# Two RWKV edits in a hybrid diffusion layer: 32x32 products that alternate between row halves, and zero-padded low parts of the small ranks

## The chip, the cores and the metric

The kernel runs on one core of a Trainium2 chip. The metric is the device time of one execution in microseconds (us). Below, PE is the matrix engine, PEld its weight loads, DVE the vector engine, ACT the scalar engine, POOL the GpSimd engine, SP the engine whose queue issues the DMAs.

## The reference

Two layers over 256 context and 512 latent tokens of width 1024. The even layer runs latent attention beside eight RWKV-7 heads of width 64, in both directions. What the change touches is the RWKV part:

```
w_log = -softplus(-(w0[d] + tanh(xw) @ w2[d])) - 0.5      # small rank 64 -> 512
a     = sigmoid(a0[d] + xa @ a2[d])                       # small rank 64 -> 512
def step(s, inp):                                         # per token, per head, per direction d
    r_t, w_t, k_t, v_t, kk_t, a_t = inp
    sa = einsum('bhij,bhj->bhi', s, -kk_t)
    s = s*w_t[:,:,None,:] + sa[...,None]*(kk_t*a_t)[:,:,None,:] + v_t[...,None]*k_t[:,:,None,:]
    return s, einsum('bhij,bhj->bhi', s, r_t)
```

Everything is float32 in and out.

## The kernel before

The token scan is done in 12 chunks of 64 tokens. In a chunk the recurrence is a unit triangular 64x64 system, and its inverse is formed ahead of the chain that walks through the chunks. The heads go in four pairs, p = 0 to 3, and two pairs share one chain, q = 0 (p 0 and 1) and q = 1 (p 2 and 3).

For each pair, `features(p)` projects r, k and v from the 1024-wide input (matmuls `acc<-h,whi` and `acc<-h,wlo`: every weight is split into a rounded high part and a low part, each in the one-pass format fp32r), then forms decay and learning rate from the small ranks. Their input `xla[n]` holds 64 rows of the high part and, in the other half, 64 rows of the low part of tanh(xw) (n = 0) or xa (n = 1). Two products make one result: `lhi` (128 rows, L626) and the weights' low part `llo` (64 rows, the half `H[n]`, L627). For 2 ranks, 2 directions and 4 pairs these are 16 accumulators, each with four matmuls: 256 and 512 columns by `lhi`, 256 and 512 by `llo`.

`rwkv_prep` multiplies the chunk matrices (`gk<-ar,bkt`) and copies what the inverse needs into `LS` and `PB`. `rwkv_inverse(p-1)` runs after it: DVE transposes `LS` into `I` (L738), POOL inverts the 32x32 diagonal blocks in 30 steps (L744, L746), DVE transposes the result into `PN` and `TT` (L751 to L754), and PE joins the two halves of each 64x64 inverse by two 32x32 products per chunk, row half and direction: `iv<-PN,PB` into bank `b`, copied by ACT to `w1` (L763), then `iv<-TT,w` into `b2`, copied to `TT` (L768), which a DMA writes to the record `sp_rec` (L770). The row halves are `Q`: rows 0 to 31 with 32 to 63, and rows 64 to 95 with 96 to 127. Before, all 12 chunks of one half stand ahead of the 12 of the other, and the copy of `b2` stands between the halves.

`rwkv_chain` then takes 12 steps for q = 0 and q = 1, each starting with loads of the record and of v (L800, L802). It overlaps with the attention's projections and heads; the rest (output projection, feed-forward, the whole odd layer) is dense matrix work from about 720 us on.

No order is written out by hand: the tile framework takes the program as written, places each instruction on its engine's in-order queue when its inputs are ready by its own cost estimate, and guards tiles by semaphores. A changed dependence in one place can therefore move instructions in others. A tile name without a number of buffers has one buffer, and a new writer waits for the last reader of the old contents.

Of the kernel before, what the change touches and what calls it, by code (L numbers as in the profile page):

```python
# [10 lines left out]
F32 = mybir.dt.float32  # L11
F32R = mybir.dt.float32r
AF = mybir.ActivationFunctionType
ALU = mybir.AluOpType
# [3 lines left out]
P = 128  # L18
# [10 lines left out]
NCH = 12  # L29
# [181 lines left out]
def hybrid_kernel(ctx: ExitStack, tc: tile.TileContext, a, out):  # L211
    nc = tc.nc
# [11 lines left out]
    def T(pool, shape, tag, bufs=1, dt=F32):  # L224
        uid[0] += 1
        return PL[pool].tile(shape, dt, tag=tag, bufs=bufs, name=f"{tag}_{uid[0]}")
# [26 lines left out]
    tt = nc.vector.tensor_tensor  # L253
# [247 lines left out]
    xla = [T("pa", [P, NTOK], f"xla{n}", 1, F32R) for n in range(2)]  # L501
# [28 lines left out]
    H = (slice(0, 64), slice(64, P))  # L530
    ALL = slice(0, P)
    SC = 96 ** -0.5
    ps = acc()
# [23 lines left out]
    ps = acc()  # L557
# [4 lines left out]
    ps = acc()  # L562
# [23 lines left out]
    for q in range(2):  # L586
        EC.append(T("misc", [P, 2, 2, NCH], f"EC{q}"))
        REC.append(tc.dram_tile([P, NCH, 2, 2, RECW], F32, name=f"sp_rec{q}"))
        VD.append([tc.dram_tile([64, NCH, 2, 2, CH], F32, name=f"sp_v{q}{m}") for m in range(2)])

    def features(p):
        r, k, v = [project(3 * p + b) for b in range(3)]
        vt = PJ()
# [16 lines left out]
                dma(dst[:, 2 + hh::-2, 1], src[:, 0:2])  # L610
                dma(dst[:, 10 + hh:3:-2, 1], src[:, 2:6])
        whi = [T("pa", [P, 2, P], f"lhi{n}", 1, F32R) for n in range(2)]
        wlo = T("pa", [P, 2, P], "llo", 1, F32R)
        for n in range(2):
            raw = T("pa", [P, 2, P], "lraw", 2)
            for m in range(2):
                dma(raw[H[m]], a["lora"][H[n], :, p * P:(p + 1) * P])
            nc.scalar.copy(whi[n], raw)
            tt(out=wlo[H[n]], in0=raw[H[n]], in1=whi[n][H[n]].bitcast(F32), op=ALU.subtract)
        sig, av = [], []  # L620
        for d in range(2):
            for n, (base, lst) in enumerate((("w0_", sig), ("a0_", av))):
                t = PJ()
                ps = acc()
                for (po, t0, nn, _) in SEG2:
                    mm(ps[:, po:po + nn], lhsT=whi[n][:, d], rhs=xla[n][:, t0:t0 + nn], start=True, stop=False)  # L626
                    mm(ps[:, po:po + nn], lhsT=wlo[H[n], d], rhs=xla[n][H[n], t0:t0 + nn], start=False, stop=True)  # L627
                act(t if d == 0 else t[:, ::-1], ps[:, PO:], AF.Sigmoid, bias=col(f"{base}{d}", p))
                lst.append(t)
        sq = PJ()  # L630
        act(sq, k, AF.Square, scale=col("k_k", p))
        ps = acc()
# [8 lines left out]
        ps = acc()  # L641
# [51 lines left out]
    Q = [(slice(64 * q, 64 * q + 32), slice(64 * q + 32, 64 * q + 64)) for q in range(2)]  # L693
# [40 lines left out]
    def rwkv_inverse(p, LS, PB):  # L734

        I = T("pp", [P, 32, 32], "I", 2)
        TT = T("pp", [P, 32, 64], "TT", 1)
        nc.vector.transpose(I.rearrange("p t s -> p (t s)"), LS.rearrange("p t s -> p (t s)"))  # L738
        Jf = T("pp", [P, 384], "w1", 2)
        eng = nc.gpsimd if INV_POOL[p] else nc.vector  # L740
        for m in range(1, 31):
            n = 31 - m
            tmp = Jf[:, :n * m].rearrange("p (t s) -> p t s", s=m)
            eng.tensor_tensor(out=tmp, in0=I[:, m + 1:, m:m + 1].to_broadcast([P, n, m]),  # L744
                              in1=I[:, m:m + 1, :m].to_broadcast([P, n, m]), op=ALU.mult)
            eng.tensor_tensor(out=I[:, m + 1:, :m], in0=I[:, m + 1:, :m], in1=tmp, op=ALU.add)  # L746
        nc.gpsimd.affine_select(out=I, in_=I, pattern=[[1, 32], [-1, 32]], compare_op=ALU.is_gt, fill=0.0,
                                base=0, channel_multiplier=0)
        nc.gpsimd.memset(I.rearrange("p t s -> p (t s)")[:, 0:1024:33], 1.0)
        PN = T("pp", [P, 32, 32], "PN", 1)  # L750
        nc.vector.transpose(PN, I.rearrange("p t s -> p s t"))  # L751
        for r0, r1 in Q:
            nc.vector.transpose(TT[r0, :, :32].rearrange("p i t -> p t i"), I[r0])
            nc.vector.transpose(TT[r1, :, 32:].rearrange("p i t -> p t i"), I[r1])  # L754
            nc.gpsimd.memset(TT[r1, :, :32], 0.0)
        for d in range(2):
            b = T("iv", [P, 512], "iv", 1)[:, :384].rearrange("p (c x) -> p c x", x=32)
            w1 = T("pp", [P, 384], "w1", 2).rearrange("p (c x) -> p c x", x=32)
            for r0, r1 in Q:
                for c in range(NCH):  # L760
                    mm(b[r1, c], lhsT=PB[r0, d * NCH + c], rhs=PN[r0, :, d * NCH + c], start=True, stop=True)
            for r0, r1 in Q:
                nc.scalar.copy(w1[r1], b[r1])  # L763
            b2 = T("iv", [P, 512], "iv", 1)[:, :384].rearrange("p (c x) -> p c x", x=32)
            for r0, r1 in Q:
                for c in range(NCH):
                    mm(b2[r0, c], lhsT=w1[r1, c], rhs=TT[r1, d * NCH + c, 32:], start=True, stop=True)
                nc.scalar.copy(TT[r0, d * NCH:d * NCH + NCH, 32:], b2[r0])  # L768
            for cs_, st_ in CMAP[d]:
                dma(REC[p // 2][:, st_, d, p % 2, 448:512], TT[:, d * NCH + cs_.start:d * NCH + cs_.stop])  # L770
# [179 lines left out]
    for tb in range(6):  # L950
        b = bank()
        n = 0
# [442 lines left out]
    ps = acc()  # L1395
# [230 lines left out]
```

## Time and profile before

| | us |
|---|---|
| median of 3 runs (2283.03 to 2285.35) | 2283.06 |
| the profiled execution | 2277.27 |
| its span, first to last instruction | 2275.6 |
| PE busy | 2103.0 (92%) |
| DVE busy | 1348.8 (59%) |
| ACT busy | 927.6 (41%) |
| POOL busy | 497.1 (22%) |

All that the change names lies between 30 and 505 us. A timeline row merges neighbours of one kind: start, time from the first start to the last end, engine, line, operation, output<-inputs, shape, count, and in brackets the idle time ahead of it with what ended it. A full float32 matmul shows as two records, an fp32r matmul as one. A matmul's recorded time includes its way through the array, so consecutive ones overlap in the record, and what one costs in a row of many is the distance of starts.

### The profile page before, as it was taken

The page shows a single profiled execution, that of the slowest core. Times are in us where ns is not written, and L with a number is a line of the kernel's source. Part 1 is how long each engine was busy: PE and PEld are TensorE (multiplying, and loading weights), DVE is VectorE, ACT ScalarE, POOL GpSimd, SP SyncE. Part 2 cuts the span into 40 slices and gives each one's busy share as a digit, 9 for nine tenths or more (in the row PEclk, how much of TensorE's full clock was granted, in tenths as well). Part 3 has the DMA queues.
Part 4 walks back from the last instruction along what each step waited for, and adds up shares of the span by engine and source line. Part 5 has one row for each costly group of instructions (what it writes and reads, how often), then busy time and mean ns, then how long its engine had stood idle before and what let it go on. Part 6 is the DMA issues. An engine that isn't in the chain of part 4 may idle for free.

```text
span 2275.6 us, 33862 instructions
## 1 busy us (share of the span) xinstructions
PE 2103.0 (92%) x13558; PEld 1654.7 (73%) x13558; DVE 1348.8 (59%) x2081; ACT 927.6 (41%) x1434; POOL 497.1 (22%) x484
## 2 busy tenths in 40 slices
PE   5988899798899999999999998898888999999997
PEld 3666668686555778888888886786565667888886
DVE  5466865666677556445354454678975556554555
ACT  4345663532245244223132335544344345332434
POOL 0027586621133010000000004342641230000000
PEclk9899899699999999999999999999888999999999
DMA  8477677659861432221211223313426032223231
GB/s 307 110 196 200 176 207 200 208 161 313 256 225 42 148 133 71 61 66 56 74 53 59 75 60 112 97 48 116 132 66 170 31 105 84 93 94 101 84 116 61
DMA packets 181069, 282.58 MB, mean 124 GB/s; under 512 B 63328, under 2 KB 118656, under 8 KB 177840
## 3 DMA queue, kind: packets, MB, share of 16 engines
q1 hardware_dynamic: 180912, 280.42, 40.7%
q8 instruction: 107, 1.75, 0.3%
q14 instruction: 50, 0.41, 0.1%
HBM read 225.43 MB, written 47.33 MB: 120 GB/s over the span
## 4 chain that ended last, share of the span: by engine, by line
PE 64%; DVE 6%; DMA 4%; ACT 4%; issue 2%; SPq 0%; DVEq 0%; POOL 0%; ACTq 0%; POOLq 0%
PE acc L267 49%; PE sd L267 3%; PE wo L267 2%; PE b L267 2%; PE ab L267 2%; PE o L267 2%; DVE E L1354 1%; DMA u<-sp_v 1%; DMA E<-sp_ac 1%; PE ax L267 1%; ACT L416 0%; DMA f<-sp_q 0%; DMA wraw<-w_out 0%; PE mb L267 0%; PE ad L267 0%
## 5 line engine op out<-in xcount | busy, mean ns | idle before, releaser
L267 PE MATMUL acc<-s,whi 128*128 128x512 f32 (+1 forms) x3104 | 762.3, 356 | 2.4 <-ACT s L463 2.4
L267 PEld LDWEIGHTS acc<-s,whi 128*128 128x128 f32 x3104 | 545.1, 188 | 94.3 <-ACT s L463 6.1
L267 PE MATMUL acc<-s,wlo 128*128 128x512 f32 (+1 forms) x1552 | 460.6, 357 | 0.0
L267 PE MATMUL acc<-h,whi 128*128 128x256 f32 (+2 forms) x1248 | 321.6, 371 | 15.4 <-ACT p L635 4.9
L325 ACT CAST whi<-wraw 128x1024 fp32r<-128x1024 f32 (+5 forms) x228 | 210.2, 923 | 284.3 <-PE acc L267 203.9
L267 PEld LDWEIGHTS acc<-s,wlo 128*128 128x128 f32 x1552 | 290.5, 188 | 46.7 <-DVE wlo L326 0.7
L267 PEld LDWEIGHTS acc<-h,whi 128*128 128x128 f32 (+1 forms) x1248 | 223.0, 196 | 67.9 <-issue 15.6
L326 DVE TENSOR_TENSOR wlo<-wraw,whi 128x1024 fp32r<-128x1024 f32 (+5 forms) x205 | 219.2, 1072 | 40.0 <-ACT whi L325 39.4
L381 DVE SCALAR_TENSOR_TENSOR s<-acc,pv,s 128x511 f32<-128x511 f32 (+1 forms) x132 | 87.0, 659 | 245.3 <-ACT s L380 244.4
L380 ACT ACTIVATE s<-acc,pv 128x512 f32<-128x512 f32 (+1 forms) x132 | 93.5, 708 | 231.8 <-PE acc L267 220.5
L484 DVE SCALAR_TENSOR_TENSOR x<-acc,mods,x 128x512 f32<-128x512 f32 (+1 forms) x136 | 79.4, 621 | 176.5 <-PE acc L267 176.4
L267 PE MATMUL acc<-h,wlo 128*128 128x256 f32 (+2 forms) x624 | 179.8, 362 | 0.0
L434 POOL TENSOR_TENSOR f<-f,f 128x768 f32<-128x768 f32 (+1 forms) x24 | 31.3, 1305 | 629.9 <-ACT f L429 622.4
L267 PEld LDWEIGHTS acc<-h,wlo 128*128 128x128 f32 (+1 forms) x624 | 120.3, 196 | 21.7 <-issue 5.2
L383 DVE SCALAR_TENSOR_TENSOR s<-acc,pv,s 128x511 f32<-128x511 f32 (+1 forms) x132 | 87.2, 660 | 4.3
L1173 POOL TENSOR_TENSOR s<-w,s 128x256 f32<-128x256 f32 x6 | 5.0, 857 | 382.4 <-ACT s L416 382.4
L387 ACT CAST s<-s 128x768 fp32r<-128x768 f32 (+1 forms) x44 | 32.0, 727 | 109.4 <-DVE s L1146 109.4
L744 POOL TENSOR_TENSOR w<-I 128x30 f32<-128x30 f32 (+14 forms) x120 | 69.8, 582 | 30.7 <-PE iv L267 12.9
L326 POOL TENSOR_TENSOR wlo<-wraw,whi 128x1024 fp32r<-128x1024 f32 x23 | 62.8, 2734 | 58.5 <-ACT whi L325 55.0
L746 POOL TENSOR_TENSOR I<-I,w 128x30 f32<-128x30 f32 (+14 forms) x120 | 71.9, 599 | 9.1
L1354 DVE TENSOR_SCALAR E<-E,acm 128x128 f32<-128x128 f32 x128 | 61.1, 546 | 16.9 <-ACT G L1351 16.9
L719 DVE TENSOR_TENSOR W<-gk,con 64x512 f32<-64x512 f32 x48 | 32.8, 683 | 55.9 <-ACT PB L718 55.5
(389 smaller groups left out, 3375.0 us busy)
## 6 DMA issues: line engine op xcount, KB each, us to landing
aw<-ada SPq DMA_DIRECT2D x96, 512.0 KB, 6.1
wraw<-up SPq DMA_DIRECT2D x88, 512.0 KB, 3.5
rec<-sp_rec SPq DMA_DIRECT2D x24, 1024.0 KB, 11.4
wraw<-w_in SPq DMA_DIRECT2D x47, 512.0 KB, 3.8
wraw<-down SPq DMA_DIRECT2D x40, 384.0 KB, 3.1
sp_rec<-tg SPq DMA_DIRECT2D x24, 384.0 KB, 3.4
E<-sp_ac SPq DMA_DIRECT2D x16, 512.0 KB, 6.6
x<-xT SPq DMA_DIRECT2D x16, 384.0 KB, 6.0
```

Of the source, the lines that this page charges most:

```text
L267: ins = nc.tensor.matmul(o, lhsT=lhsT, rhs=rhs, start=start, stop=stop, skip_group_check=shared)
L325: nc.scalar.copy(hi[:, :kt], raw[:, :kt])
L326: (eng or tt)(out=lo[:, :kt], in0=raw[:, :kt], in1=hi[:, :kt].bitcast(F32), op=ALU.subtract)
L380: act(o[rows, t0:t0 + n], ps[rows, po:po + n], AF.Identity, scale=w1, bias=b)
L381: stt(out=o[rows, t0 + 1:t0 + n], in0=ps[rows, po:po + n - 1], scalar=w0, in1=o[rows, t0 + 1:t0 + n], op0=ALU.mult, op1=ALU.add)
L383: stt(out=o[rows, t0:t0 + n - 1], in0=ps[rows, po + 1:po + n], scalar=w2, in1=o[rows, t0:t0 + n - 1], op0=ALU.mult, op1=ALU.add)
L387: nc.scalar.copy(hi, src)
L484: stt(out=x[:, t0:t0 + n], in0=ps[:, po:po + n], scalar=mods[:, c6 * 8 + m, c:c + 1], in1=x[:, t0:t0 + n], op0=ALU.mult, op1=ALU.add)
L719: tt(out=w[hk], in0=b[hk].rearrange("p c (a t) -> p c a t", a=2), in1=mk[hk].rearrange("p (a t) -> p a t", a=2).unsqueeze(1).to_broadcast( ...
L744: eng.tensor_tensor(out=tmp, in0=I[:, m + 1:, m:m + 1].to_broadcast([P, n, m]), in1=I[:, m:m + 1, :m].to_broadcast([P, n, m]), op=ALU.mult)
L746: eng.tensor_tensor(out=I[:, m + 1:, :m], in0=I[:, m + 1:, :m], in1=tmp, op=ALU.add)
L1354: ts(out=e[:, h], in0=e[:, h], scalar1=acm[:, c, h0 + h:h0 + h + 1], scalar2=0.0, op0=ALU.subtract, op1=ALU.min)
```

## The change

Three edits. The 32x32 products of both kinds loop over chunks outside and over row halves inside, so that neighbours belong to different halves; both copies of `b2` now stand behind all 24 products. The low parts of the small ranks get two tiles `llo0` and `llo1` of 128 rows, whose unused half POOL sets to zero once at the start; the product then takes all 128 rows (the zero rows add nothing). The staging tile `lraw` goes from two buffers to one.

```
+    llo = [T("pa", [P, 2, P], f"llo{n}", 1, F32R) for n in range(2)]
+    for n in range(2):
+        nc.gpsimd.memset(llo[n][H[1 - n]].bitcast(F32), 0.0)
...
-        wlo = T("pa", [P, 2, P], "llo", 1, F32R)
         for n in range(2):
-            raw = T("pa", [P, 2, P], "lraw", 2)
+            raw = T("pa", [P, 2, P], "lraw", 1)
             for m in range(2):
                 dma(raw[H[m]], a["lora"][H[n], :, p * P:(p + 1) * P])
             nc.scalar.copy(whi[n], raw)
-            tt(out=wlo[H[n]], in0=raw[H[n]], in1=whi[n][H[n]].bitcast(F32), op=ALU.subtract)
+            tt(out=llo[n][H[n]], in0=raw[H[n]], in1=whi[n][H[n]].bitcast(F32), op=ALU.subtract)
...
-                    mm(ps[:, po:po + nn], lhsT=wlo[H[n], d], rhs=xla[n][H[n], t0:t0 + nn], start=False, stop=True)
+                    mm(ps[:, po:po + nn], lhsT=llo[n][:, d], rhs=xla[n][:, t0:t0 + nn], start=False, stop=True)
...
-            for r0, r1 in Q:
-                for c in range(NCH):
+            for c in range(NCH):
+                for r0, r1 in Q:
                     mm(b[r1, c], lhsT=PB[r0, d * NCH + c], rhs=PN[r0, :, d * NCH + c], start=True, stop=True)
             for r0, r1 in Q:
                 nc.scalar.copy(w1[r1], b[r1])
             b2 = T("iv", [P, 512], "iv", 1)[:, :384].rearrange("p (c x) -> p c x", x=32)
+            for c in range(NCH):
+                for r0, r1 in Q:
+                    mm(b2[r0, c], lhsT=w1[r1, c], rhs=TT[r1, d * NCH + c, 32:], start=True, stop=True)
             for r0, r1 in Q:
-                for c in range(NCH):
-                    mm(b2[r0, c], lhsT=w1[r1, c], rhs=TT[r1, d * NCH + c, 32:], start=True, stop=True)
                 nc.scalar.copy(TT[r0, d * NCH:d * NCH + NCH, 32:], b2[r0])
```

The order of instructions changes on every engine from the first `lraw` on. Three places matter below. The first is DVE's queue at the features of p = 0; the `llo` rows are the low parts of p = 1, `p_852` or `p_855` is the running sum of the decay that everything after it needs. Before:

```order
L619 TENSOR_TENSOR llo_1358<-lraw_1359,lhi_203_1356 64x256
L640 SCALAR_TENSOR_TENSOR p_841<-f_631,pv_71,f_693 128x768
L661 SCALAR_TENSOR_TENSOR p_852<-scanm_116,p_805 128x768
L661 SCALAR_TENSOR_TENSOR p_874<-scanm_116,p_819 128x768
L619 TENSOR_TENSOR llo_1358<-lraw_1364,lhi_204_1357 64x256
L644 TENSOR_TENSOR f_755<-acc_843,f_755 128x768
L638 SCALAR_TENSOR_TENSOR p_833<-f_693,nkc_348,p_833 128x768
```

and now:

```order
L623 TENSOR_TENSOR llo_96_573<-lraw_1361,lhi_204_1359 64x256
L644 SCALAR_TENSOR_TENSOR p_844<-f_635,pv_71,f_697 128x768
L665 SCALAR_TENSOR_TENSOR p_855<-scanm_116,p_808 128x768
L665 SCALAR_TENSOR_TENSOR p_877<-scanm_116,p_822 128x768
L648 TENSOR_TENSOR f_759<-acc_846,f_759 128x768
L642 SCALAR_TENSOR_TENSOR p_836<-f_697,nkc_348,p_836 128x768
L682 SCALAR_TENSOR_TENSOR p_808<-p_815,p_836 128x768
L682 SCALAR_TENSOR_TENSOR p_822<-p_829,p_836 128x768
L623 TENSOR_TENSOR llo_97_574<-lraw_1366,lhi_205_1360 64x256
L683 TENSOR_TENSOR p_808<-p_808,p_855 128x768
```

The first subtraction stays ahead of the sums, but its tile is now read by rank n = 0 alone; the second one moved four places back. The second place is PE's queue at the join of p = 2 and the first chain step of q = 0 (`b_3934`, `b_3955`); `acc_5414` is the sum of squares of the attention's kv rank. Before:

```order
L267 MATMUL iv_3226<-PN_3218,PB_2214 32x32 x24
L267 MATMUL iv_3254<-TT_3153,w_455_3227 32x32 x12
L728 MATMUL gk_3145<-con_70,bkt_2939 128x128 x4
L267 MATMUL iv_3254<-TT_3153,w_455_3227 32x32 x12
L267 MATMUL acc_5414<-f_5417,ones_72 128x256
L267 MATMUL acc_5414<-f_5417,ones_72 128x512
L267 MATMUL iv_3282<-PN_3218,PB_2214 32x32 x24
L267 MATMUL b_3934<-u_3911,rec_3910 64x64 x8
L267 MATMUL iv_3310<-TT_3153,w_458_3283 32x32 x12
L267 MATMUL b_3934<-rs_3943,rec_3910 64x64 x8
L267 MATMUL iv_3310<-TT_3153,w_458_3283 32x32 x12
```

and now:

```order
L732 MATMUL gk_3145<-con_70,bkt_2939 128x128 x4
L267 MATMUL iv_3226<-PN_3218,PB_2215 32x32 x24
L267 MATMUL b_3934<-u_3911,rec_3910 64x64 x8
L267 MATMUL iv_3254<-TT_3153,w_453_3227 32x32
L267 MATMUL b_3934<-rs_3943,rec_3910 64x64 x8
L267 MATMUL iv_3254<-TT_3153,w_453_3227 32x32 x23
L267 MATMUL acc_5414<-f_5417,ones_72 128x256
L267 MATMUL acc_5414<-f_5417,ones_72 128x512
L267 MATMUL b_3955<-u_3911,rec_3910 64x64 x8
L267 MATMUL iv_3282<-PN_3218,PB_2215 32x32 x24
```

The chain's first step stands between the two kinds of joins, the second kind runs as one piece but for its first product, and the kv sum stands behind it. The third place is DVE's queue at the same time: `I_3393<-LS` is the start of the inverse of p = 3, `PN_3218` and `TT_3153` the transposes of p = 2. Before:

```order
L751 STREAM_TRANSPOSE PN_3218<-I_3152 128x1024
L753 STREAM_TRANSPOSE TT_3153<-I_3152 32x32x32
L754 STREAM_TRANSPOSE TT_3153<-I_3152 32x32x32
L753 STREAM_TRANSPOSE TT_3153<-I_3152 32x32x32
L754 STREAM_TRANSPOSE TT_3153<-I_3152 32x32x32
L719 TENSOR_TENSOR W_3122<-gk_3123,con_70 64x512
L722 TENSOR_TENSOR tg_3121<-gk_3123,con_70 64x4x64
L434 TENSOR_TENSOR f_5417<-f_5415,f_5417 128x768
L738 STREAM_TRANSPOSE I_3393<-LS_2963 128x1024
```

and now:

```order
L723 TENSOR_TENSOR W_3122<-gk_3123,con_70 64x512
L726 TENSOR_TENSOR tg_3121<-gk_3123,con_70 64x4x64
L742 STREAM_TRANSPOSE I_3393<-LS_2963 128x1024
L723 TENSOR_TENSOR W_3122<-gk_3134,con_70 64x512
L726 TENSOR_TENSOR tg_3121<-gk_3134,con_70 64x4x64
L755 STREAM_TRANSPOSE PN_3218<-I_3152 128x1024
L757 STREAM_TRANSPOSE TT_3153<-I_3152 32x32x32
L758 STREAM_TRANSPOSE TT_3153<-I_3152 32x32x32
L757 STREAM_TRANSPOSE TT_3153<-I_3152 32x32x32
L758 STREAM_TRANSPOSE TT_3153<-I_3152 32x32x32
```

The transposition that starts p = 3 moved ahead of the five of p = 2.

## Rows read from the trace of the kernel before

**Rows 1.** The page: span, and busy time, share and instructions of PE.

```profile
span 2275.6 us, 33862 instructions
PE 2103.0 (92%) x13558; PEld 1654.7 (73%) x13558; DVE 1348.8 (59%) x2081; ACT 927.6 (41%) x1434; POOL 497.1 (22%) x484
```

**Rows 2.** Stretches: length; busy PE, PEld, DVE, ACT, POOL; granted clock; DMA share; GB/s.

```profile
90.00:250.00 160.00, 137.54 (x778) 96.56 (x777) 96.28 (x121) 83.75 (x153) 70.89 (x83) 0.89 0.68 181
250.00:404.00 154.00, 145.62 (x1158) 114.08 (x1157) 100.37 (x114) 77.45 (x146) 106.18 (x149) 0.95 0.72 187
404.00:448.00 44.00, 32.44 (x365) 25.92 (x366) 26.87 (x33) 23.70 (x43) 23.02 (x40) 0.59 0.79 238
448.00:500.00 52.00, 51.53 (x483) 43.37 (x481) 36.33 (x44) 21.46 (x43) 19.68 (x31) 0.88 0.46 141
```

**Rows 3.** Groups by form on PE, 0 to 700 us: records, busy, mean ns.

```profile
L267 PE MATMUL iv<-PN,PB 32*32 32x32 f32 x384 | 21.5, 228 | 0.3 <-DVE PN L751 0.3
L267 PE MATMUL iv<-TT,w 32*32 32x32 f32 x384 | 18.5, 210 | 5.1 <-ACT TT L768 3.6 <-ACT w L763 1.5
L267 PE MATMUL acc<-xla,llo 64*128 64x512 f32 x16 | 8.8, 551 | 0.0
```

**Rows 4.** PE's timeline: one accumulator of the small ranks, and what follows.

```profile
312.79 0.38 PE L267 MATMUL acc<-xla,lhi 128*128 128x256 f32 x1
313.10 0.38 PE L267 MATMUL acc<-xla,llo 64*128 64x256 f32 x1
...
314.27 0.55 PE L597 MATMUL bkp<-con,f 128*128 128x128 f32 x3
```

**Rows 5.** PE's timeline: 128-row projections, then a run of 64-row products.

```profile
395.94 0.85 PE L267 MATMUL acc<-h,whi 128*128 128x256 f32 x4
396.63 0.51 PE L267 MATMUL acc<-h,wlo 128*128 128x256 f32 x2
397.41 1.71 PE L267 MATMUL gk<-ar,bkt 64*128 64x128 f32 x16
```

**Rows 6.** PE's timeline: joins of p = 3 and p = 2, chain products among them.

```profile
431.24 1.12 PE L267 MATMUL b<-rs,rec 64*64 64x64 f32 x16 [1.44 <-ACT rs L816]
...
488.64 2.65 PE L267 MATMUL iv<-PN,PB 32*32 32x32 f32 x48
...
495.17 0.94 PE L267 MATMUL iv<-TT,w 32*32 32x32 f32 x24
496.04 0.68 PE L267 MATMUL b<-rs,rec 64*64 64x64 f32 x16
```

**Rows 7.** PE's timeline: second half of a TT product, p = 0.

```profile
263.69 1.48 PE L267 MATMUL iv<-TT,w 32*32 32x32 f32 x24 [3.60 <-ACT TT L768]
```

**Rows 8.** Timelines of ACT and DVE, features of p = 0.

```profile
105.80 1.70 ACT L628 ACTIVATE p<-acc,pv 128x768 f32<-128x768 f32 x2
112.35 0.42 DVE L619 TENSOR_TENSOR llo<-lraw,lhi 64x256 fp32r<-64x256 f32 x1 [12.77 <-PE acc L267]
113.62 3.39 DVE L661 TENSOR_TENSOR_SCAN p<-scanm,p 128x768 f32<-128x768 f32 x2
```

**Rows 9.** Timelines of DVE and POOL, transposes of p = 2, start of p = 3.

```profile
408.76 1.91 DVE L751 STREAM_TRANSPOSE PN<-I 128x1024 f32<-128x1024 f32 x1
416.47 1.90 DVE L754 STREAM_TRANSPOSE TT<-I 32x1024 f32<-32x1024 f32 x1
420.33 1.23 DVE L738 STREAM_TRANSPOSE I<-LS 128x1024 f32<-128x1024 f32 x1
422.37 0.25 POOL L744 TENSOR_TENSOR w<-I 128x30 f32<-128x30 f32 x1 [8.72 <-DVE W L719]
```

**Rows 10.** The chain that ended last, 500 to 517 us: start, us, what.

```profile
501.41 0.48 ACT TT L768
507.49 9.20 DMA u<-sp_v
516.83 0.30 PE b L267 x2
```

## The prediction

> **What bounds the kernel now.** I read the page first: PE is busy for 2103.0 of 2275.6 us, 92% [rows 1], so time taken off PE is worth something wherever PE is not waiting for others. Then the stretches, since the change lies in the RWKV part alone [rows 2]. From 90 to 250 us PE is busy for 137.54 of 160 (86%), from 250 to 404 for 145.62 of 154 (95%), from 404 to 448 for 32.44 of 44 (74%), with a mean granted clock of 0.59, that is, mostly at 1.2 GHz; from 448 to 500 for 51.53 of 52. The reader is to see four different limits: up to 250 us a mixture of PE and waits for ACT, DVE and POOL; up to 404 PE; then a hand-over, where the last inverses, the start of the chain and the attention's norm wait for each other; then PE again. The forms say how much the change can reach [rows 3]: 21.5 and 18.5 us of recorded time for the two kinds of joins (384 records each, two for a product, so 8 groups of 24 products of either kind), and 16 accumulators of the small ranks. Last I read timelines for the spacing of neighbours, the waits and the chain that ended last [rows 4 to 10].
>
> **Part 1, padding.** In a warm accumulator of the small ranks the four matmuls take from 312.79 to 314.27, 1.48 us start to start [rows 4]. Four matmuls with the same 256, 512, 256 and 512 columns, all of 128 rows, take from 395.94 to 396.63, 0.69 us [rows 5]. The zero rows add no columns, so the padded accumulator should run like the second: 0.79 us less. Whether the 64 rows cost this or the alternation between 128 and 64 rows need not be known: the change takes both away. 16 accumulators x 0.79 = 12.6 us of PE. Twelve of them lie before 250 us, where PE is only 86% busy and part of what it saves turns into longer waits for ACT and DVE; four lie at 305 to 325 us, where PE is the limit. I take two thirds, 8.4 us; the bounds are 0 and 12.6. The two memsets on POOL stand at the program's start, long before the first use of `llo`, and cost nothing; were POOL late there, it would be by two short instructions of 64 rows.
>
> **Part 2, alternation.** A PN group of 48 records takes 2.65 us (0.055 per record), a TT group of 24 takes 0.87 from 495.17 to 496.04 (0.036) [rows 6], with the same 32 columns and no alternation either. So the TT products already run at a pace that PN could at best reach. 48 x 0.036 = 1.74 us, 0.9 less per PN group. Does alternation help? The nearest row is `b<-rs,rec`: 64 columns, row halves alternating, both halves into one bank, 16 records in 0.68 us, 0.042 per record [rows 6]. The run of 128-column products, one half after the other, needs 1.71/16 = 0.107 per record [rows 5], so 0.053 for 64 columns; the alternating ones are faster, hence they overlap. At 1.2 GHz the same products take 1.12/16 = 0.070 [rows 6] and a cold TT group 1.48/24 = 0.062 [rows 7], more than PN's 0.055: a cold PN group gains nothing. Of the 8 PN groups the two of p = 2 lie in the stretch at 0.59 [rows 2, 9], and I count one of p = 3 as slow too. That leaves 5 x 0.9 = 4.5 us; 3.5 on the path, four of the five lying where PE is 95% busy or in the stretch to 404. Bounds: 0 and 8 x 0.9 = 7.2. A loss from changing the half at each product is excluded by the row of `b<-rs`, which changes at each of its 8 products and needs 0.68 us in all.
>
> A rule speaks against this term. The Trainium skill, "TensorEngine Tiling (Array Packing)", section "Restrictions and Gotchas", says that different row tiles cannot write to the same PSUM bank at the same time; both halves of `b` are in one bank. By that rule the alternating PN products would still go one after the other, and the term would be 0 instead of 3.5. The row of `b<-rs`, with its 0.042 against 0.053, does not look like that, though its tiles are of 64 rows; I go with the row and keep the other as a rival.
>
> **Part 3, the second join in one piece.** Before, the second half of a TT product waits until ACT has copied the first half: PE stood 3.60 us [rows 7], and all idle time before TT products is 5.1 us [rows 3]. Now no copy stands between. In exchange the first copy, 0.48 us [rows 10], comes after all 24 products, and both copies run in a row. 3.60 less two copies across the stretch, and some of it late for other reasons: I take 2 us. Bounds: 5.1 gained, or 8 x 0.48 = 3.8 lost if every copy is late on the path.
>
> **Part 4, DVE's queue and the single staging buffer.** At p = 0 DVE stands 12.77 us before the first low part of the next pair, until 112.35 [rows 8], because the one tile was read by the last small-rank product of either rank. Behind it are the sums, at 113.62, although ACT had delivered their input by 107.50 (105.80 + 1.70). Now the first subtraction waits for rank 0 alone, so one accumulator less: at most 6.1 us (113.62 - 107.50), probably 1. Against that the second low part now stands in front of the product that the chunk matrices wait for, it needs a cast that ACT does after the exponentials, and the second load waits until `lraw` is free, with the loads of `bkt` and `aw` behind it on SP's queue. I set this at 1 us lost, so 0 for both; bounds 6.1 gained, 3.4 lost (8 subtractions of 0.42 us, all in front of something urgent).
>
> **Part 5, the hand-over.** DVE's five transposes of p = 2 ran from 408.76 to 418.37 (416.47 + 1.90), and only then, at 420.33, the transpose that lets POOL start p = 3, at 422.37 [rows 9]. Now that one goes first. p = 3 may begin up to 9.6 us earlier (418.37 - 408.76), and it decides when the record for q = 1 is written (501.41), its load ends and the products of q = 1 begin (516.83) [rows 10]. But the transposes of p = 2 now wait for the last chunk matrix of p = 3, and PE's queue has the chain's first step between the joins of p = 2 and the kv sum behind them: up to 9.6 us more of standing at 1.2 GHz. I take 0, with bounds of 9.6 both ways.
>
> **Sum.** -8.4 - 3.5 - 2 + 0 + 0 = -13.9 us. Against the profiled execution (2277.27, of which 1.67 lie around the span) that is 2263.4. The median of the runs shown is 5.8 above the profiled one; taken off the median, 2283.06 - 13.9 = 2269.2. I predict 2269.
>
> **Rivals.**
> - *PN stays at its pace.* For: with the same 32 columns PN needs 0.055 and TT 0.036 [rows 6], so something other than columns holds PN, and alternation need not lift it; and the rule on banks. Against: the pace of `b<-rs`. Then -10.4: 2272.7.
> - *The gain is not on the path.* POOL's inverses (106.18 us busy from 250 to 404 [rows 2]) or ACT set the pace up to 404, and PE's saved time becomes waiting, but for part 3: 2281. Against: PE is 95% busy there, POOL 69%, DVE 65%.
> - *The hand-over gets worse.* The transposes of p = 2 start 9.6 us later, PE stands in front of them, and the attention's norm, which now is behind them in PE's queue, makes everything to 500 us late; p = 3's earlier start is not used, since PE at 51.53 of 52 has no room for it. Upstream gives its lower 4 us: +5.6, 2288.7. It decides when PE's idle time between 404 and 448 rises from 11.6 us by more than the features gained.
> - *More than the sum.* Nearly all of PE's saving counts (12.6 + 7.2) and p = 3's start brings 6 to 9 us at 517: -26 to -29, about 2256.
>
> **How the numbers follow.** Forecast, 2263 to 2275: 0.42. PN at its pace: 0.12. Not on the path: 0.17. Hand-over worse: 0.11. More: 0.18. About 0.2% (4.6 us) can be told from no change. Faster by more than that are the forecast, the first and the last, and a little of the second: 0.73; slower, the third and a small part of the second: 0.12; same: 0.15. For 8 in 10 I leave out the worse hand-over and the lower half of the last case: 2256 to 2284.
>
> **What would show it.** Right: the `llo` products appear as 128 rows, and an accumulator takes about 0.7 us start to start at 2.4 GHz; PN groups of 48 records near 1.7 to 2.0 us; no wait of PE for ACT's copy of the TT products (L773) inside a group; the stretch up to the last chunk matrix shorter by 8 to 14 us; PE's busy time lower. Wrong: PN still at 2.65; the last chunk matrix of p = 3 no earlier, with longer waits of PE for ACT; more idle between that point and the first full attention work; or the products of q = 1 beginning no earlier than 516.83.

## The result and the profile after

The kernel after takes 2267.32 us (median of 5 runs, 2264.21 to 2271.00), the kernel before 2283.06 (5 runs, 2275.15 to 2288.36): a ratio of 0.994, with a 95% interval of 0.9916 to 0.9964. That is 13.7 us of 2283.06; the two medians themselves lie 15.7 us apart. The profiled execution, the fastest of the five, has a span of 2262.3 us. Of all executions below, one stands apart, 10349.73 us of the kernel of experiment 9, and its ratio leaves it out. The page says, against [rows 1]:

```profile
span 2262.3 us, 33884 instructions
PE 2076.5 (92%) x13558; PEld 1640.9 (73%) x13558; DVE 1346.3 (60%) x2081; ACT 928.3 (41%) x1434; POOL 506.2 (22%) x486
```

PE is busy for 26.5 us less and the span is 13.3 us shorter: half of what PE saved arrived in these two executions. The same four stretches as in [rows 2] (length; busy PE, PEld, DVE, ACT, POOL; granted clock; DMA share; GB/s):

```profile
90.00:250.00 160.00, 134.85 (x844) 100.16 (x842) 101.35 (x123) 88.39 (x163) 72.30 (x83) 0.91 0.70 186
250.00:404.00 154.00, 136.98 (x1116) 107.75 (x1116) 100.28 (x118) 80.52 (x153) 113.78 (x152) 0.92 0.75 201
404.00:448.00 44.00, 32.55 (x423) 24.84 (x424) 33.29 (x36) 23.95 (x38) 28.27 (x38) 0.70 0.66 206
448.00:500.00 52.00, 45.07 (x509) 37.98 (x508) 33.44 (x46) 17.78 (x39) 14.50 (x29) 0.90 0.59 173
```

Between 250 and 404 us PE is no longer 95% busy but 89%. The forms on PE, 0 to 700 us, against [rows 3]:

```profile
L267 PE MATMUL iv<-PN,PB 32*32 32x32 f32 x384 | 12.6, 228 | 7.1 <-DVE PN L755 7.1
L267 PE MATMUL iv<-TT,w 32*32 32x32 f32 x384 | 9.7, 203 | 8.5 <-DVE TT L758 7.8 <-ACT w L767 0.7
L267 PE MATMUL acc<-xla,llo 128*128 128x512 f32 x16 | 7.0, 439 | 0.0
```

Both joins take a little over half the busy time (21.5 to 12.6, 18.5 to 9.7), while the mean of a single PN record stays at 228 ns, so it is the overlap that grew, not the single product that became shorter. In exchange the idle time before them rose: 0.3 to 7.1 and 5.1 to 8.5, now for DVE's transposes. PE's timeline (start, length, engine, line, output<-inputs, count, idle time before) shows the steps, against [rows 4, 6, 7]:

```profile
310.12 0.39 PE L267 MATMUL acc<-xla,lhi 128*128 128x256 f32 x1 [0.30 <-ACT p L632]
310.34 0.28 PE L267 MATMUL acc<-xla,llo 128*128 128x256 f32 x1
...
310.93 0.37 PE L267 MATMUL acc<-xla,lhi 128*128 128x256 f32 x1
...
357.80 1.53 PE L267 MATMUL iv<-PN,PB 32*32 32x32 f32 x48
363.61 0.95 PE L267 MATMUL iv<-TT,w 32*32 32x32 f32 x48
...
406.88 1.56 PE L267 MATMUL iv<-PN,PB 32*32 32x32 f32 x48 [3.48 <-DVE PN L755]
...
469.79 0.28 PE L267 MATMUL iv<-TT,w 32*32 32x32 f32 x2 [2.28 <-DVE TT L758]
473.54 1.48 PE L267 MATMUL iv<-TT,w 32*32 32x32 f32 x46 [3.47 <-DVE TT L758]
```

An accumulator starts at 310.12 and the next at 310.93: 0.81 us instead of 1.48. A PN group takes 1.53 instead of 2.65, and at the low clock (406.88) 1.56, where before had this row:

```profile
412.84 2.72 PE L267 MATMUL iv<-PN,PB 32*32 32x32 f32 x48
```

A whole TT product of 48 records takes 0.95, as much as half of one before. The last two rows of the timeline of after show the price: two records run, and then PE waits 3.47 us for the fifth transpose, because the alternating product needs both row halves of `TT` at its second step.

Where the time went is best read between three points: the last product by `lhi` of the small ranks (324.0 before, 311.2 after), the last join, and the last product that reads a buffer named `rec`, where the input of the output projection stands by then. After it everything is dense matrix work. First before, then after:

```profile
500.02 0.94 PE L267 MATMUL iv<-TT,w 32*32 32x32 f32 x24
...
816.41 0.51 PE L267 MATMUL acc<-rec,whi 128*128 128x256 f32 x2
```
```profile
485.39 0.95 PE L267 MATMUL iv<-TT,w 32*32 32x32 f32 x48
...
808.20 0.52 PE L267 MATMUL acc<-rec,whi 128*128 128x256 f32 x2
```

The last join is 14.6 us earlier, but from there to the last `rec` product it takes 322.8 us instead of 316.4: 6.4 us are given back in a stretch in which no instruction was edited. The stretch isn't of one kind: the chain's last product by the record starts at 697.83 before and 697.25 after, so there all but 0.6 us is gone, and the output projection, with which the dense work begins, starts at 749.11 (later than the 720 us given for the kernel before) and 735.30, 13.8 us earlier again. From the last `rec` product to the last product of the kernel the two profiles differ by 5.6 us, in work that is the same; over all the kernels below this remainder lies between 1442.5 and 1449.0 us, so I count it as scatter. Of the 13.3 us only 8.2 are thus accounted for up to the last `rec` product.

### The profile page after: what moved, and what is told of

Same layout as the page of the kernel before. It is cut to its first block, busy times and chain, and to the rows that moved or that the text cites. A ratio compares the mean times of both kernels' runs of the same rounds, so it can differ in the third digit from the quotient of the medians.

```text
span 2262.3 us, 33884 instructions
## 1 busy us (share of the span) xinstructions
PE 2076.5 (92%) x13558; PEld 1640.9 (73%) x13558; DVE 1346.3 (60%) x2081; ACT 928.3 (41%) x1434; POOL 506.2 (22%) x486
## 4 chain that ended last, share of the span: by engine, by line
PE 65%; DVE 6%; ACT 5%; DMA 5%; issue 3%; POOL 1%; SPq 0%; DVEq 0%; ACTq 0%; POOLq 0%
PE acc L267 49%; PE sd L267 3%; PE o L267 3%; PE wo L267 2%; PE ab L267 2%; PE b L267 2%; DMA u<-sp_v 1%; DVE E L1359 1%; DMA aw<-ada 1%; POOL I L750 1%; PE ax L267 1%; PE ad L267 1%; POOL w L748 1%; DMA E<-sp_ac 1%; ACT L416 1%
## 5 line engine op out<-in xcount | busy, mean ns | idle before, releaser
L750 POOL TENSOR_TENSOR I<-I,w 128x30 f32<-128x30 f32 (+14 forms) x120 | 76.7, 639 | 9.0
L1359 DVE TENSOR_SCALAR E<-E,acm 128x128 f32<-128x128 f32 x128 | 61.2, 546 | 14.6 <-ACT G L1356 14.6
```

The lines of the kernel that those rows point to most:

```text
L1359: ts(out=e[:, h], in0=e[:, h], scalar1=acm[:, c, h0 + h:h0 + h + 1], scalar2=0.0, op0=ALU.subtract, op1=ALU.min)
```

## The experiments

Two theories. **A:** what PE saves counts, in part; each edit has its own share. **Order:** the edits change the order that the framework writes out, and this order decides by more than the edits save. Times are medians; the ratio is to runs of the kernel before on the same chip (median 2280.43, 2279.23 and 2280.13 in the three rounds of experiments). A difference in us between an experiment and after is that of their ratios to before; by the two 95% intervals it is uncertain by 6 to 7 us. A profile shows one execution, and those of one kernel spread (before from 2268.88 to 2296.47 in the first round), so points read from profiles scatter too. Below, "the stretch" is the time from the last join to the last `rec` product in the profiled execution.

**1. Only the padding.** Both loops and the copies as before, the rest as after.

```
-            for c in range(NCH):
-                for r0, r1 in Q:                  # both joins
+            for r0, r1 in Q:
+                for c in range(NCH):
```

> The padded low parts of the kernel after, both joins as in the kernel before. Theory A (matrix-engine time is on the path in part: padding saves 16 x 0.7 = 11 us of it, the joins 8 x (1.1 + 0.9) = 16 us, and 13 of the 27 us arrived): 5 to 6 us faster than before, and the first chunk products (141.5 us after, 149.6 before) at 141 to 143 us, as after. Theory B (the waits that the new dependences removed, not the matrix-engine time): 8 to 13 us faster, since the two low-part tiles and the order of the vector engine's queue are kept. Theory C (alternation alone brings the end forward; what padding saves early is lost in later waits): within 2 us of before.

Measured: 2286.23 us, ratio 1.0023 (1.0006 to 1.0041): slower, which no theory expected. The first chunk products are at 144.1 us (before 149.6), the last join at 494.4, 5.6 us earlier than before. But the stretch takes 334.9 us, 18.5 more than before.

**2. Only the alternation.** The kernel before with both loops turned and the copies behind.

> The kernel before with both joins alternated and the second one in one piece; low parts of 64 rows in one tile as before. Theory A: 7 to 9 us faster than before, joins of 48 records at 1.53 us (PN) and 0.95 us (TT), and the first chunk products no earlier than 149 us. Theory B: within 3 us of before, since the dependences of the low parts are the old ones. Theory C: 12 to 15 us faster, the same time as after.

Measured: 2302.11 us, ratio 1.0090 (1.0074 to 1.0106): all three theories failed. The first chunk products stand at 149.6 as expected, the joins at 1.5 and 0.95 us, the last join at 497.8, 2.2 us earlier than before. Then:

```profile
497.81 0.95 PE L267 MATMUL iv<-TT,w 32*32 32x32 f32 x48
...
842.60 0.51 PE L267 MATMUL acc<-rec,whi 128*128 128x256 f32 x2
```

The stretch takes 344.8 us, 28.4 more than before, with no edited instruction in it. A part of it in rows: 540 to 580 us in before, then here, and three waits of PE here (total, times, longest), 500 to 780 us, which come to 0.5, 1.6 and 0.2 us in before.

```profile
540.00:580.00 40.00, 36.75 (x563) 26.42 (x565) 30.40 (x65) 12.48 (x27) 8.36 (x7) 1.00 1.04 296
```
```profile
540.00:580.00 40.00, 28.31 (x402) 19.92 (x401) 20.71 (x44) 7.65 (x16) 1.28 (x1) 0.79 1.00 320
```
```profile
PE b L267 <- DVE u L823: 7.4, 6, 3.3
PE ax L267 <- ACT qh L387: 5.6, 1, 5.6
PE ax L267 <- DVE nl L1011: 5.4, 4, 2.3
```

PE now stands in front of the chain's and the attention's products, and from 540 to 580 us its clock is lower (0.79 instead of 1.00). A comparison with another order of instructions thus measures the order as well as the edit. From here on I looked for edits that leave the order alone.

**3. Low parts of 64 rows, all else as after.** On every engine the instructions stand in the order of after.

```
-  mm(..., lhsT=llo[n][:, d], rhs=xla[n][:, t0:t0 + nn], ...)
+  mm(..., lhsT=llo[n][H[n], d], rhs=xla[n][H[n], t0:t0 + nn], ...)
```

> The kernel after, but the products by the low parts take 64 rows again; the two tiles, the one staging buffer, the two memsets and the alternated joins stay. Theory A: 5 to 6 us slower than after (accumulators of the small ranks 1.4 to 1.5 us start to start instead of 0.8, first chunk products at 146 to 149 us). Theory B: within 2 us of after, first chunk products at 143 us or earlier, because the vector engine's wait of 12.77 us for the one tile is gone all the same.

Measured: 2278.40 us, 0.9983 (0.9966 to 0.9999), against 0.9940 for after: the padding is worth 0.43%, 9.8 us, more than A's 5 to 6, and near the 16 x 0.67 = 10.7 us that it saves PE at 2.4 GHz. B (the dependences alone) is out by the time. In the profiles the two kernels are further apart: the first PN group starts at 260.3 against 244.0, 16.3 us, and the last `rec` product still 16.6 later. But the profiled execution of this kernel (2283.75) was the slowest of its 12 and that of after the fastest of its 5. What differs most is PE's clock. Stretches of this kernel, then of after (columns as above):

```profile
164.00:168.00 4.00, 2.12 (x15) 1.71 (x17) 3.58 (x6) 2.52 (x6) 0.00 (x0) 0.90 0.81 239
168.00:192.00 24.00, 24.00 (x92) 15.92 (x91) 11.87 (x18) 16.32 (x33) 4.56 (x2) 0.50 0.51 122
```
```profile
160.00:168.00 8.00, 7.36 (x39) 6.25 (x38) 4.23 (x8) 4.27 (x11) 0.00 (x0) 0.57 0.61 159
168.00:184.00 16.00, 11.41 (x73) 7.30 (x71) 10.54 (x14) 15.20 (x27) 4.44 (x2) 1.00 0.73 187
184.00:192.00 8.00, 6.59 (x24) 5.46 (x28) 3.27 (x3) 6.70 (x9) 8.00 (x11) 0.57 0.31 89
```

With 64 rows PE is at 1.2 GHz for 24 us in a row here, although it is busy all the time; with 128 rows twice for about 8. That isn't the work of the 64 rows alone. The kernel of experiment 9 runs the same instructions in the same order up to the first PN product, also with 64 rows, and its profile has two short stretches instead:

```profile
164.00:176.00 12.00, 11.51 (x50) 8.45 (x50) 5.68 (x11) 6.41 (x17) 0.00 (x0) 0.57 0.63 161
188.00:196.00 8.00, 5.60 (x18) 4.84 (x19) 3.24 (x4) 7.67 (x10) 8.00 (x10) 0.58 0.43 140
```

Its first PN group starts at 255.1, its first chunk products at 144.8 (147.4 here, 149.6 before). Seven profiles with 128 rows, whose instructions are the same up to the inverse of p = 0, have the PN group at 243.8 to 247.5 and the chunk products at 141.3 to 144.1. So at the first chunk products the dependences bring 2.2 to 4.8 us and the padding the rest, and 5 us between two profiles can be scatter. What unpadded products cost more at the low clock is shown where the neighbours are the same, first in this kernel, then in after:

```profile
169.66 0.56 PE L267 MATMUL acc<-xla,lhi 128*128 128x256 f32 x1
...
172.11 1.11 PE L732 MATMUL gk<-con,bkt 128*128 128x128 f32 x4
```
```profile
164.11 0.56 PE L267 MATMUL acc<-xla,lhi 128*128 128x256 f32 x1
...
165.54 1.05 PE L732 MATMUL gk<-con,bkt 128*128 128x128 f32 x4
```

An accumulator takes 2.45 us with 64 rows and 1.43 padded, 1.02 us less instead of the 0.67 at 2.4 GHz (granted clock 0.50 in both places). Why the clock falls and comes back when it does, the profiles don't show.

**4. Chunk products of both row halves into two open banks.**

```
+  bs = [gbank()... for _ in range(2)]
+  for c in range(GC):
+      for par in range(2): mm(bs[par][:, c], ...)       # gk<-ar,bkt
```

> The kernel after, in which the 384 records of the chunk products of ar and bkt (64 rows, 128 columns, 0.107 us per record) also alternate between the row halves, into two banks that are open at once. Theory A (products of different row halves overlap, and half of what the matrix engine saves arrives): 0.06 to 0.085 us per record, 8 to 18 us less busy time, 4 to 9 us faster than after (2258 to 2263). Theory B (waits set the time here; both banks are read later): 0 to 4 us slower than after at the same or a lower busy time. Theory D (128 columns keep the array full, the overlap exists only where a product is shorter than its weight load): 0.107 us per record stays, and the time is that of after.

Measured: 2289.07 us, 1.0030 (1.0014 to 1.0045). Inconclusive for what it was made for: the framework put the four products of one bank ahead of those of the other again, so nothing alternates: 16 records take 1.71 us as before, and ACT's first copy out of them starts 1.19 us after the first record, as in after. The question whether wider products overlap stays open. But it tells of the order: the last join is at 488.0, 2.6 us behind after, and the stretch takes 344.3 us.

**5. After, PN not alternated** (the PN loop of before; order of after).

> The kernel after, but the first join (PN) takes all chunks of one row half and then those of the other, as before; every engine's instructions stand in the same order as after, but for the 24 products within each join. Theory A (the matrix-engine time of the first join is on the path): PN groups of 48 records at 2.65 us instead of 1.53, 9 us more busy time, 5 to 9 us slower than after. Theory B (the first join stands between waits for the transposes, which in the kernel after cost 7.1 us of idle time, so a longer join shortens the next wait): 0 to 3 us slower.

Measured: 2276.45 us, 0.9982 (0.9967 to 0.9998): 0.42%, 9.6 us slower than after, with 9.1 us more busy time in PN (21.7). Theory A holds; as far as the interval tells, all of PN's saving arrives here. The last join is 10.5 us later (495.9).

**6. Before, PN alternated** (order of before).

> The kernel before with the first join (PN) alternated and nothing else; the order of instructions on every engine is that of before, but within each join. Theory A: PN groups at 1.53 to 1.56 us instead of 2.65, 5 to 9 us faster than before. Theory B: 0 to 3 us faster, since the copies and the second join behind it are waited for all the same. If both this and the kernel with nothing alternated but padded lows stand within 3 us of before, while both joins alternated stood 20 us above it, the order that came with the second join's change decides, not its products.

Measured: 2280.07 us, 0.9999 (0.9978 to 1.0020): nothing, though the saving on PE is the same:

```profile
L267 PE MATMUL iv<-TT,w 32*32 32x32 f32 x384 | 17.7, 206 | 6.1 <-ACT TT L768 4.1 <-ACT w L763 1.9 <-DVE TT L754 0.2
L267 PE MATMUL iv<-PN,PB 32*32 32x32 f32 x384 | 12.6, 228 | 0.3 <-DVE PN L751 0.3
```

The second group starts 3.4 us earlier (267.8), the last product by `lhi` of the small ranks 0.2 us later (324.2). In between the clock takes it back in this execution; 300 to 320 us in before, and here:

```profile
300.00:320.00 20.00, 17.36 (x119) 13.10 (x118) 11.98 (x23) 12.59 (x31) 17.80 (x29) 1.00 0.84 264
```
```profile
300.00:320.00 20.00, 17.46 (x94) 12.83 (x93) 10.79 (x20) 10.83 (x27) 17.72 (x29) 0.74 0.75 229
```

The same busy time, but 0.74 of the clock instead of 1.00, and fewer instructions done. So theory B has the outcome, by another cause than it names. The last sentence of the expectation came true only in part: this kernel stands at before, the padded one 0.23% above it.

**7. 64 rows, grouped:** first both products by `lhi`, then both by `llo`. In short:

```
-  for seg: mm(lhi, seg); mm(llo 64 rows, seg)
+  for seg: mm(lhi, seg)
+  for seg: mm(llo 64 rows, seg)
```

> The kernel after with low parts of 64 rows (as in the experiment with the two tiles at 64 rows), but in each small-rank accumulator both products by the high part come first and then both by the low part: two changes between 128 and 64 rows per accumulator instead of four; the order is otherwise that of after. Theory S (the change of row count costs the time, 0.2 us each at 2.4 GHz): 1.05 to 1.15 us per accumulator start to start instead of 1.48, and a time about halfway between the 64-row kernel and after, 5 to 6 us slower than after. Theory R (a 64-row product itself is slower than one of 128 rows): 1.4 to 1.5 us, 10 us slower than after.

Measured: 2274.29 us, 0.9970 (0.9952 to 0.9988), 6.8 us slower than after. An accumulator:

```profile
316.80 0.62 PE L267 MATMUL acc<-xla,lhi 128*128 128x256 f32 x2 [0.30 <-ACT p L632]
317.35 0.61 PE L267 MATMUL acc<-xla,llo 64*128 64x256 f32 x2
317.89 0.62 PE L267 MATMUL acc<-xla,lhi 128*128 128x256 f32 x2
```

1.09 us, between 1.48 (four changes of row count) and 0.81 (none): theory S. A change of row count costs 0.14 to 0.2 us at 2.4 GHz, (1.09 - 0.81)/2 and (1.48 - 1.09)/2; the 64 rows themselves cost nothing that shows. That neighbours now share their weights doesn't explain it: the weights are loaded as often as before (13558 PEld records in both).

**8. PN laid out contiguously** (order of after).

```
-  nc.vector.transpose(PN, I.rearrange("p t s -> p s t"))            # rhs=PN[r0, :, j]
+  nc.vector.transpose(PN.rearrange("p i s -> p s i"), I.rearrange("p t s -> p s t"))   # rhs=PN[r0, j]
```

> The kernel after, with PN laid out so that the 32 columns of a product are contiguous, as they are in TT (after and before read them at a stride of 32 elements); order as after. Theory T (the stride holds the first join at 0.031 us per record where the second needs 0.020): PN groups at 0.95 us instead of 1.53, 4.6 us less busy time, 1 to 4 us faster than after. Theory U (the stride costs nothing; something else tells the joins apart): 1.53 us stays, and the time is that of after.

Measured: 2265.55 us, 0.9941 (0.9919 to 0.9962): the time of after. Theory T is right on the pace (0.95 us for 48 records, 260.38) and wrong on the gain: PN's busy time falls by 3.6 us, the idle time before PN and TT rises from 15.6 to 16.9, and the last join stays where it was (485.3).

**9. The order of after with the old work:** experiments 3 and 5 together.

> The kernel after with low parts of 64 rows and the first join (PN) not alternated: the order of after on every engine, with what these two edits save put back. Theory A (the savings add: 10 us for the padding, 9 us for the first join, measured one at a time in this order): 2284 to 2288 us, that is 4 to 8 us slower than before, so the order of after would by itself be the worse one. Theory C (both savings shorten the same low-clock stretches, so that the second one put back costs little): 2277 to 2281 us, the time of before.

Measured: 2284.93 us, 1.0016 (1.0002 to 1.0030). Theory A: put back together the two cost 0.76%, put back singly 0.43 and 0.42%; they nearly add. With the old accumulators and the old PN products the new order, its new waits and the faster TT product are together slower than before, by 0.16%.

**10. TT not alternated**, both copies behind all 24 products; the order moves a little.

> The kernel after, but the second join (TT) takes the 12 chunks of one row half and then those of the other; both copies stay behind all 24. The order of the other instructions also moves, above all behind the last join. Theory A (the matrix-engine time of the join): 1.8 to 1.9 us per 48 records instead of 0.95, the products of q = 1 begin 3 to 8 us later than after (501.0), and the end is as much later. Theory O (the order behind the last join decides): whatever the beginning of q = 1, the stretch from there to the last product by rec takes either about 305 us (as before 303.7, after 307.2) or about 327 us (as in the kernels with only the padding, only the joins, and both banks opened at once), so the total stands near 2271 or near 2292 us.

Measured: 2275.80 us, 0.9974 (0.9961 to 0.9986), 7.7 us slower than after. 48 records take 1.60 us (269.01), not 1.8 to 1.9. The last join is 3.1 us later than after (the longer join fills part of the wait for the transposes, 3.0 us instead of 8.5), the stretch 330.2 us, 7.4 longer: neither of theory O's two numbers. In the profile, then, most of the loss stands in a stretch whose order moved, and the 7.7 us are not the join's alone.

**11. PN contiguous, not alternated**, one execution.

> The kernel after with PN laid out contiguously and its products not alternated: one look at the pace of the first join. Theory V (stride and alternation are two costs that add): 1.8 to 1.9 us per 48 records, as the second join before (2 x 0.94). Theory W (alternation only hides the stride): 0.95 to 1.0 us.

Measured: 2266.49 us, the time of after as far as one execution tells; the last join stands at 485.1, as in after.

```profile
357.21 1.60 PE L267 MATMUL iv<-PN,PB 32*32 32x32 f32 x48
...
406.46 2.58 PE L267 MATMUL iv<-PN,PB 32*32 32x32 f32 x48 [3.98 <-DVE PN L755]
```

Theory W is out. Theory V is right that there are two costs, but the pace is 1.60 instead of 1.8 to 1.9, and they multiply rather than add: 2.65 us with neither edit, 1.53 with alternation, 1.60 with contiguous columns, 0.95 with both. Contiguous columns alone do for PN what the alternation does. At the low clock the layout hardly matters (2.58 and 1.49).

**12. One transpose for what the second join needs.** With 8's layout:

```
+  nc.vector.transpose(TT[:, :, 32:].rearrange("p i t -> p t i"), I)     # all 128 partitions
   for r0, r1 in Q:
       nc.vector.transpose(TT[r0, :, :32]..., I[r0])
-      nc.vector.transpose(TT[r1, :, 32:]..., I[r1])
```

> The kernel after with PN contiguous, and the transposes that the second join needs made by one instruction of 128 partitions instead of two of 32 each, ahead of the two others; what it writes into the other row half is overwritten by the joined part. DVE has one instruction of 1.9 us less per pair of heads, and PE's operand is there after the second transpose instead of after the fifth. Theory A: PE's idle time before the second join falls from 8.5 us to under 3, the products of q = 1 begin at 494 to 500 us instead of 501.0, and the kernel is 3 to 8 us faster than after (2259 to 2264). Theory O: the order behind the last join changes, the stretch from there to the last product by rec grows from 307 to 320 us or more, and the kernel is 8 to 20 us slower than after.

Measured: 2260.84 us, 0.9909 (0.9891 to 0.9926), the fastest kernel of this study, 0.31% or 7 us below after. The forms on PE, 0 to 700 us, then DVE's transposes of the last pair, then PE's last join:

```profile
L267 PE MATMUL iv<-PN,PB 32*32 32x32 f32 x384 | 8.7, 200 | 1.4 <-DVE PN L755 1.4
L267 PE MATMUL iv<-TT,w 32*32 32x32 f32 x384 | 8.6, 200 | 1.5 <-ACT w L767 1.5
```
```profile
461.99 1.91 DVE L756 STREAM_TRANSPOSE TT<-I 128x1024 f32<-128x1024 f32 x1
463.75 3.88 DVE L758 STREAM_TRANSPOSE TT<-I 32x1024 f32<-32x1024 f32 x2
```
```profile
480.41 0.95 PE L267 MATMUL iv<-TT,w 32*32 32x32 f32 x48
```

The idle time before TT falls from 8.5 to 1.5 us, the last join is 5.0 us earlier than after, and the stretch, though its order changed, is 322.3 us: theory A in the size of the gain. The products of q = 1, though, begin at 500.2 and not at 494 to 500: they wait for the load of v. The gain can't be put down to the missing wait alone: the order moved on every engine from about 250 us on (the third PN group starts at 325.5 instead of 344.3), and with the wait gone the layout of experiment 8 may count too. The three were not separated.

**The stretch behind the last join**, over all kernels:

| order | kernels | us from last join to last `rec` product |
|---|---|---|
| of before | before, 6 | 316.4, 315.7 |
| of after | after, 3, 5, 7, 8, 9, 11 | 322.8, 322.6, 324.5, 323.2, 323.4, 321.3, 322.7 |
| others | 1; 2; 4; 10; 12 | 334.9; 344.8; 344.3; 330.2; 322.3 |

Same order, same length within 4 us, wherever the join stood (485 to 502 us); other orders, up to 30 us more. The kernels of experiments 2 and 4 differ in the padding, in the chunk products and by 10 us in the time of the last join, but in the stretch their order on PE is the same but for 9 of 2979 records, and they take 344.8 and 344.3 us. No kernel has an edited instruction in it, so the order sets it. Both theories hold, then, each in its stretch: what PE saves counts up to the last join, in so far as the clock and the waits let it, and behind it the order decides.

## Why the prediction was right, point by point

The time (2269 against 2267.32) is right; the sum behind it is right in one term, and errors of opposite sign cancel in the others. That the time came out within 2 us is luck.

- **Padding, -8.4.** Mechanism and size hold: accumulators at 0.81 us, 9.8 us on the path (experiment 3), uncertain by 6 to 7. What I left open is settled: the change of row count costs, not the 64 rows (7). I had counted accumulators at 2.4 GHz only; at 1.2 GHz one saves 1.02 us instead of 0.67.
- **Alternation, -3.5, bounds 0 to 7.2.** This term was mis-sized. The step that failed is "So the TT products already run at a pace that PN could at best reach." The 0.87 us from the TT group to the chain's product [rows 6] also holds the change to another kind of product, and products that don't alternate don't show the pace of those that do: 0.95/48 = 0.020 us per record instead of 0.036. So TT gained as well, PN gained more, and "a cold PN group gains nothing" is wrong too: 2.72 to 1.56. PN was worth 9.6 us in the order of after (5), though nothing in the order of before (6), and TT, with a moved order, 7.7 (10). The Trainium skill, "TensorEngine Tiling (Array Packing)", section "Restrictions and Gotchas", says that different row tiles cannot access one PSUM bank at the same time, which would have left PN at 2.65; the trace disagrees, 1.53 with both halves in one bank, each in its own partitions.
- **TT join in one piece, -2.** Wrong in sign for the wait: the 3.60 us for ACT's copy [rows 7] are gone, but the product now needs both halves' transposes, and the idle time before it rose from 5.1 to 8.5 us. I had asked what is late next on ACT and not on DVE. Experiment 12 removes this wait; with the new layout and another order it is 7 us faster than after.
- **DVE's queue and the staging buffer, 0.** Inside its bounds. DVE's wait at p = 0 [rows 8] fell from 12.77 to 7.71 us, and the sums start at 107.18 instead of 113.62. With 64 rows and the same dependences the wait is 10.29 and the sums start at 111.63 (3) and 109.68 (9), so the dependences bring 2.0 to 3.9 of these 6.4 us and the padding the rest; whether their part reaches the end, no run shows.

```profile
105.91 0.42 DVE L623 TENSOR_TENSOR llo<-lraw,lhi 64x256 fp32r<-64x256 f32 x1 [7.71 <-ACT lhi L622]
106.25 1.00 DVE L644 SCALAR_TENSOR_TENSOR p<-f,pv,f 128x768 f32<-128x768 f32 x1
107.18 3.39 DVE L665 TENSOR_TENSOR_SCAN p<-scanm,p 128x768 f32<-128x768 f32 x2
```

- **Hand-over, 0, bounds 9.6 both ways.** The start of p = 3 did move ahead of the transposes of p = 2 (402.61, where 420.33 stood in [rows 9]), and PE did wait 3.48 us for them at 406.88. The last join is 14.6 us earlier, the last accumulator 12.8: 1.8 gained. I stopped the account at 517 us, though. Behind the last join the order costs 6.4 us more than before, and it could as well have cost 28 (experiment 2). None of the rivals named this place.

```profile
402.61 1.25 DVE L742 STREAM_TRANSPOSE I<-LS 128x1024 f32<-128x1024 f32 x1 [0.45 <-ACT LS L721]
404.91 1.91 DVE L755 STREAM_TRANSPOSE PN<-I 128x1024 f32<-128x1024 f32 x1
```

- **The sum.** Put back one at a time in the order of after, padding, PN and TT cost 9.8 + 9.6 + 7.7 = 27.1 us, about what PE's busy time fell by; 13.7 arrived. I put the missing 13 down to the order and the waits that came with it, which is argued more than shown. For it: with two of the three savings put back the new order stands 3.6 us above before (9), and with TT's 7.7 added, an estimate, 11. Of this 6.4 lie behind the last join. Against a closer account: each share is uncertain by 6 to 7 us, and most of TT's stands in a stretch whose order moved. The three put back together were not tried.

## What to carry to other kernels

Before an edit is timed, see whether it leaves the order of instructions on every engine as it was: if so, a difference beyond the scatter is the edit's; if not, compare point by point up to the last edited instruction, and expect the stretch behind it to move with the order (here up to 30 us). Read a point from more than one profile: the same instructions stood 5 us apart in two executions. Group products by the number of rows, or pad them to one number; alternate small products between row halves, and then see that the operands of both halves are ready at the same time. A pace read from a group that doesn't overlap is no floor for one that does.

## What was not expected of the hardware

- Four 32x32 float32 layouts of the same work, 48 records: 2.65, 1.60, 1.53 and 0.95 us (strided or contiguous columns, one half after the other or alternating). A stride of 32 elements in the streamed operand costs a factor of 1.6 at 2.4 GHz and 1.05 at 1.2 GHz (1.56 against 1.49). The Trainium skill, "SBUF — State Buffer", section "Door 1: The DMA port swizzle (why `[64,N]` ≈ `[32,N]`)", says that each access which crosses to a new 16-byte line pays a penalty; the trace agrees at 2.4 GHz (0.95 to 1.53 us), though only one stride was run, and at 1.2 GHz next to nothing is left of it.
- A change between products of 128 and of 64 rows costs 0.14 to 0.2 us at 2.4 GHz; at 1.2 GHz, between the same neighbours, an accumulator with four changes takes 2.45 us and one without 1.43, so about 0.26 each.
- PE stayed at 1.2 GHz for 24 us while it was busy all the time (168 to 192 us in experiment 3), after 4 us in which it was busy for 2.12. Another execution of the same instructions (9) had two stretches of about 12 and 8 us instead, at a mean granted clock of 0.57 and 0.58: the clock differs between executions of one order.
